# First mixer's gate projection in seven half-size products; norm weights as columns; one pair's k products placed later

## The chip, the cores and the metric

The kernel runs on one core of a Trainium2 chip. Its engines run side by side, each through its own list of instructions in order: TensorE (PE: matrix products; PEld is the load of its stationary operand), VectorE (DVE), ScalarE (ACT), GpSimd (POOL) and SyncE (SP, which here only issues transfers). They wait for one another through semaphores. The metric is the device time of one execution in microseconds, as the median of several runs.

## The reference

Two residual layers over 512 tokens of width 1024, in float32. Layer 0 mixes tokens by gated linear attention (the first mixer), layer 1 by gated DeltaNet (the second mixer). Behind each mixer stands a convolutional feed-forward network, and behind each of these four parts a layer normalisation. What matters here is the first mixer:

```python
def gla_mixer(x, w_in, w_gk2, b_gk, norm_w, w_out):
    proj = x @ w_in                       # 1024 -> 512 + 512 + 1024 + 1024 + 16
    q, k, v, gate, gk_lr = jnp.split(proj, ...)
    ...
    o = rms_norm(gla_chunked(qc, kc, vc, gc), norm_w)     # 4 heads of 256; norm_w has 256 numbers
    o = from_head_chunks(o).astype(x.dtype)
    return (o * jax.nn.silu(gate)) @ w_out
```

The second mixer ends in the same way, with 8 heads of 128 and a norm weight of 128 numbers. It also forms k k^T per head, and from that a triangular inverse in chunks.

## The kernel before, in words

**Precision.** A float32 product is made of three products in a faster format (fp32r). Each operand is split into a high part (`wh`, `xh`, `yh`: a cast on ScalarE) and a low part (`wl`, `xl`, `yl`: the difference to the cast, on VectorE), both by `split_out` (L591, recorded at L592). Then high x high, high x low and low x high go into one accumulator (`tm_terms`). A matmul of the large projections has a stationary operand of 128x128 and a moving one of 128x512.

**Weights.** A plan lists the weight pieces in the order of use. Each piece is a tile of 128x1024 (two blocks of 128 rows by 512 columns), loaded by SP's queue into one of three buffers named `raw`, and split into one of four pairs `wh`, `wl`. The look-ahead says how many pieces are split before they are used: two in most stages.

**The first mixer.** The projections come in the order q and k per head, then v, then the gates, then the output projection. For v and for the gates, `x_tm` calls `tm_half` once per half of the 1024 columns: four accumulators, one for each 128 tokens, and four pieces of weights; each piece is used in 24 matmuls (4 token blocks, 2 row blocks, 3 terms). That is 192 matmuls for the gates. When a block is complete, `gates` (L984) takes silu on ScalarE (L991) and multiplies by the norm weight on VectorE (L993), which lies repeated on all 128 partitions as `gla_nw`. `finish` (L1198), one task per half, waits for four gate tiles `sg` and two heads, multiplies each gate tile with the heads' output and its inverse norm (L1207, 128x256 at a time), and hands them to `split_y` (L976): four transposes per tile on TensorE (`yT`), and the split into `yh` and `yl`. These are the stationary operands of the output projection.

**The order.** The code is a recorder: one main thread issues the large projections, and after each group of matmuls `pump` resumes those side tasks whose time by an estimated clock has come. A task is `spawn`ed with a delay. A scheduler behind it keeps each engine's dependencies. So a changed delay or an added task moves instructions on an engine, not only in the text.

**A form that the kernel has elsewhere.** The output projections of the feed-forward networks are computed in the Strassen-Winograd manner, here called fold: the matrices are cut in two by two quarters, seven products of sums of quarters replace eight, and the names `b11`, `b21`, `t1`, `t2`, `b22`, `t3`, `t4` are the quarters or sums of the weights, `a11`, `a12`, `w1`, `v2`, `v4`, `v3`, `a22` those of the other operand.

**The second mixer's k.** The projections of the heads come by pairs; `k_done` (L1352) runs the convolution of a k head, and for each pair spawns `k_task`: the products k k^T (`pg`: four matmuls of 128x128 per head), with a delay of `CONV_DELAY` (6.0), and `FIRST_CONVS` (2.0) more for the first two pairs. From `pg`, through `am`, comes the inverse: a long chain on VectorE, then `dinvt` in DRAM, from which SP loads tiles `T` for the products `V`.

Of the kernel before, what the change touches and what calls it, by code (L numbers as in the profile page):

```python
# [15 lines left out]
P = 128  # L16
D = 1024
S = 512
# [12 lines left out]
FOLD = [(n, FOLD_NEW[n], *FOLD_ALL[n]) for n in ("b11", "b21", "t1", "t2", "b22", "t3", "t4")]  # L31
LN_EPS = 1e-5
# [3 lines left out]
GROUPS = ((0, 8), (8, 16), (16, 22))  # L36
SLOTS = 45
# [26 lines left out]
class Trunk:  # L64
# [3 lines left out]
    def __init__(self, ctx, tc):  # L68
# [15 lines left out]
        self.stage("gla", SLOTS)  # L84
# [24 lines left out]
        self.late = []  # L109
# [151 lines left out]

    @staticmethod
    def in_slots(item):
        return item[0] == "tm" and item[5]

    def issue(self, item):
# [6 lines left out]
        if item[0] == "fold":  # L273
            return self.issue_fold(*item[1:])
        raw = self.rp.tile([P, 1024], F32, name=self.uid("raw"), tag="raw")
# [8 lines left out]
        else:  # L284
            _, w, row, n, col, _ = item
            used = n * S
            nc.sync.dma_start(
# [15 lines left out]
        if self.issued == 0:  # L303
            self.pieces = [lambda cols=cols: split(cols) for cols in pieces]
        elif self.issued < 4:
            self.opening(*split(pieces[0]))
        else:
            parts = split(pieces[0])
            for ins, other in zip(parts, self.after):
                self.behind(ins, other)  # L310
# [64 lines left out]

    def prefetch(self):
# [9 lines left out]
    def load_ahead(self, until):  # L386


        self.loaded = max(self.loaded, self.issued)
        while self.loaded < min(len(self.plan), until) and self.plan[self.loaded][0] == "fold":  # L390
            _, group, _, quarter, i = self.plan[self.loaded]
            if quarter:
                self.fold_load(group, quarter, i)
            self.loaded += 1
# [249 lines left out]
    def load_x(self, x):  # L644
# [44 lines left out]
        def second():  # L689
# [5 lines left out]
            for t, row in self.late:  # L695
                nc.gpsimd.tensor_copy(t[:, :1], self.xl[:, NC - 1, S - 1:].bitcast(F32))
                nc.gpsimd.dma_start(t, row.partition_broadcast(P))

# [277 lines left out]
    def split_y(self, y, hf, sg):  # L976
        for tb in range(NTB):
# [3 lines left out]
            self.split_out(*t, ps)  # L981
            self.set(("y", tb, hf), 1.5)

    def gates(self, nw, width, sg):  # L984

        nc = self.nc
        r = S // width
        for hf in range(2):
            def done(tb, ps, hf=hf):
                t = self.slot("sg")  # L990
                nc.scalar.activation(t, ps, AF.Silu)  # L991
                t3 = t.rearrange("p (r d) -> p r d", r=r)
                nc.vector.tensor_mul(t3, t3, nw.unsqueeze(1).to_broadcast([P, r, width]))  # L993
# [6 lines left out]
    def gla_plan(self, w_in, w_out):  # L1000
# [5 lines left out]
        for base in (1024, 2048):  # L1006
            for hf in range(2):
                for cp in range(NC // 2):
                    self.plan_tm(w_in, 2 * cp * P, 2, base + hf * S)
        self.plan_out(w_out, 0, NC, TAIL)  # L1010

    def gla_consts(self, w_gk2, b_gk, norm_w):
# [16 lines left out]
        self.gla_nw = self.own([P, 256], "gla_nw")  # L1029
        self.late.append((self.gla_nw, norm_w))  # L1030
# [9 lines left out]
        self.spawn(self.columns([(b_gk.rearrange("(n p) -> n p", p=P), 4, self.b_gk)]), 12.0)  # L1040

    def gla(self, li, g, b):
# [155 lines left out]
        def finish(hf):  # L1198
            for tb in range(NTB):
# [3 lines left out]
            for tb in range(NTB):  # L1203
# [5 lines left out]
            yield 2.4  # L1209
            self.split_y(y, hf, sg)  # L1210

        for hd in range(GH):
            self.spawn(core(hd))
        for hf in range(2):
# [5 lines left out]
            self.x_tm(v_done)  # L1220
        for hf in range(2):
            self.spawn(finish(hf))
        self.gates(self.gla_nw, 256, sg)
# [26 lines left out]
    def gdn_consts(self, conv_w, a_log, dt_bias, norm_w):  # L1250
# [3 lines left out]
        self.gdn_nw = self.keep([P, P], "gdn_nw")  # L1254
        self.late.append((self.gdn_nw, norm_w))
# [15 lines left out]
    def gdn(self, li, g, b):  # L1271
# [371 lines left out]
        def finish(hf):  # L1643
# [10 lines left out]
            self.split_y(y, hf, sg)  # L1654
# [13 lines left out]
        self.gates(self.gdn_nw, P, sg)  # L1668
# [79 lines left out]
```

## Time and profile before

| | |
|---|---|
| median of 3 runs | 1238.53 us (1238.46 to 1238.58) |
| the profiled execution | 1238.69 us, span 1237.0 us |
| TensorE busy | 1225.5 us, 99% of the span, 6566 matmuls |
| VectorE, ScalarE, GpSimd busy | 912.5, 587.2, 123.7 us |
| DMA | 130.72 MB, 106 GB/s on average |
| granted TensorE clock | 0.998 |

The span is that of the recorded instructions; the execution is longer by what lies around it. In the rows of a profile, L197 is the line where a matmul is recorded and L214 that of a transpose; the operand names stand as out<-in. A row of a group gives the count, the busy time and the mean duration, then the idle time before it and what ended that. A row of the timeline begins with the start and the duration. A row of windows gives, for a stretch, the busy time of PE, PEld, DVE, ACT and POOL, then the granted clock, the share of the DMA engines and GB/s. Matmuls overlap: their duration is longer than the distance from one to the next.

### The profile page before, as it was taken

The numbers are of one execution on the slowest core, as the hardware profiler recorded it, in microseconds if no ns is written. First come the engines' busy times: TensorE is split into PE (matmuls) and PEld (weight loads), VectorE is DVE, ScalarE is ACT, GpSimd is POOL, SyncE is SP. The second block draws the span as 40 slices with busy tenths as digits, with TensorE's granted clock in tenths as the row PEclk, the third lists the DMA queues.
The fourth block names the chain that finished last, engine by engine and source line by source line (L and its number), as shares of the span: only waits on it lengthen the run. The fifth ranks groups of instructions, "written<-read, shape, count | busy, mean of one in ns | idle before, by whom it ended". The sixth has DMA issues, their size and how long they took to land.

```text
span 1237.0 us, 17216 instructions
## 1 busy us (share of the span) xinstructions
PE 1225.5 (99%) x6566; PEld 1035.1 (84%) x6566; DVE 912.5 (74%) x1546; ACT 587.2 (47%) x1067; POOL 123.7 (10%) x161
## 2 busy tenths in 40 slices
PE   9999999999999999999999999999999999999997
PEld 8888888988888888888988888988988888888886
DVE  4863556589966895667599965679589966796667
ACT  4654434644434443455676545534644434443440
POOL 4000000062000000001023030100053000000000
PEclk9999999999999999999999999999999999999999
DMA  7422225342353214333264241335342263223321
GB/s 208 111 79 68 69 86 162 111 137 68 103 170 102 68 52 119 119 99 108 69 171 120 85 134 36 91 114 154 106 152 84 60 201 97 86 85 102 106 66 68
DMA packets 169410, 130.72 MB, mean 106 GB/s; under 512 B 16232, under 2 KB 139946, under 8 KB 169328
## 3 DMA queue, kind: packets, MB, share of 16 engines
q1 hardware_dynamic: 164240, 120.47, 32.8%
q0 software_dynamic: 3888, 8.50, 2.4%
q8 instruction: 51, 0.84, 0.3%
q10 hardware_dynamic: 1200, 0.66, 0.2%
q14 instruction: 31, 0.25, 0.1%
HBM read 123.82 MB, written 5.78 MB: 105 GB/s over the span
## 4 chain that ended last, share of the span: by engine, by line
PE 97%; ACT 1%; DVE 1%; DMA 0%; issue 0%; POOL 0%; SPq 0%; DVEq 0%; ACTq 0%
PE fm L197 52%; PE tm L197 23%; PE fold L197 12%; PE o L197 2%; PE xT L214 1%; PE V L197 1%; PE pq L197 1%; PE vn L197 1%; PE yT L214 1%; DMA h<-in_x_dram 0%; PE qs L197 0%; PE s L197 0%; PE ks L197 0%; PE ds L197 0%; PE sa L197 0%; PE qT L214 0%
## 5 line engine op out<-in xcount | busy, mean ns | idle before, releaser
L197 PE MATMUL fm<-xh,wh 128*128 128x512 f32 (+2 forms) x1104 | 402.3, 367 | 0.7 <-ACT xh L592 0.7
L197 PE MATMUL fm<-xl,wh 128*128 128x512 f32 (+2 forms) x1104 | 400.0, 365 | 0.0
L197 PE MATMUL fm<-xh,wl 128*128 128x512 f32 (+1 forms) x1080 | 392.8, 366 | 0.0
L592 DVE TENSOR_TENSOR wl<-raw,wh 128x1024 fp32r<-128x1024 f32 (+1 forms) x161 | 200.8, 1249 | 171.7 <-ACT wh L592 171.6
L592 ACT CAST wh<-raw 128x1024 fp32r<-128x1024 f32 (+1 forms) x162 | 168.6, 1043 | 247.8 <-PE fm L197 141.3
L197 PEld LDWEIGHTS fm<-xh,wh 128*128 128x128 f32 (+1 forms) x1104 | 206.9, 188 | 33.9 <-ACT xh L592 0.9
L197 PEld LDWEIGHTS fm<-xl,wh 128*128 128x128 f32 (+1 forms) x1104 | 207.0, 188 | 32.8 <-DVE xl L592 0.2
L197 PEld LDWEIGHTS fm<-xh,wl 128*128 128x128 f32 x1080 | 202.7, 189 | 33.0
L863 DVE SCALAR_TENSOR_TENSOR conv<-fm,ffn_cw,conv 128x511 f32<-128x511 f32 x112 | 83.5, 745 | 8.9 <-ACT conv L861 7.4
L197 PE MATMUL fold<-wh,fh 128*128 128x512 f32 x224 | 87.6, 391 | 0.0
L197 PE MATMUL fold<-wl,fh 128*128 128x512 f32 x224 | 87.4, 390 | 0.0
L197 PE MATMUL fold<-wh,fl 128*128 128x512 f32 x224 | 87.2, 389 | 0.0
L592 ACT CAST wh<-b 128x1024 fp32r<-128x1024 f32 x48 | 49.6, 1052 | 60.6 <-PE fold L197 25.8
L197 PE MATMUL tm<-wh,xh 128*128 128x512 f32 x192 | 78.2, 408 | 0.0
L197 PE MATMUL tm<-wh,xl 128*128 128x512 f32 x192 | 75.1, 391 | 0.0
L197 PE MATMUL tm<-wl,xh 128*128 128x512 f32 x192 | 74.8, 389 | 0.0
L881 ACT ACTIVATE conv<-conv 128x512 f32<-128x512 f32 x44 | 27.8, 632 | 80.7 <-DVE conv L863 80.7
L790 POOL TENSOR_TENSOR h<-h,gb 128x512 f32<-128x512 f32 x16 | 28.2, 1783 | 334.2 <-DMA gb<-in_ln_g_dram 227.9
L592 DVE TENSOR_TENSOR wl<-b,wh 128x1024 fp32r<-128x1024 f32 x48 | 57.8, 1218 | 2.3 <-ACT wh L592 2.3
L1266 DVE SCALAR_TENSOR_TENSOR conv<-fm,gdn_cw,conv 128x511 f32<-128x511 f32 (+2 forms) x72 | 52.7, 743 | 2.0 <-ACT conv L1264 1.5
L197 PEld LDWEIGHTS fold<-wh,fh 128*128 128x128 f32 x224 | 42.0, 188 | 9.8 <-DVE h L952 1.2
L197 PEld LDWEIGHTS fold<-wl,fh 128*128 128x128 f32 x224 | 42.0, 188 | 9.4 <-DVE wl L592 0.8
(323 smaller groups left out, 1852.7 us busy)
## 6 DMA issues: line engine op xcount, KB each, us to landing
raw<-in_ffn_w_in_dram SPq DMA_DIRECT2D x88, 512.0 KB, 3.8
raw<-in_gdn_w_in_dram SPq DMA_DIRECT2D x32, 512.0 KB, 4.1
raw<-in_ffn_w_out_dram SPq DMA_DIRECT2D x28, 512.0 KB, 3.7
b<-in_ffn_w_out_dram SPq DMA_DIRECT2D x24, 512.0 KB, 4.9
raw<-in_gla_w_in_dram SPq DMA_DIRECT2D x23, 512.0 KB, 3.7
raw<-in_gla_w_out_dram SPq DMA_DIRECT2D x8, 512.0 KB, 3.6
raw<-in_gdn_w_out_dram SPq DMA_DIRECT2D x8, 512.0 KB, 3.8
h<-in_x_dram SPq DMA_DIRECT2D x8, 256.0 KB, 5.8
```

The source lines that it names most:

```text
L197: t = self.nc.tensor.matmul(out, a, b, start=start, stop=stop, skip_group_check=joined)
L214: t = self.nc.tensor.transpose(out, a, self.ident[:n, :n])
L592: return self.nc.scalar.copy(dst_h, src), self.nc.vector.tensor_sub(dst_l, src, dst_h)
L790: nc.gpsimd.tensor_mul(h[hf], h[hf], gb[hf])
L863: nc.vector.scalar_tensor_tensor(a[:, d:], ps[:, :S - d], tap(2 - d), a[:, d:], ALU.mult, ALU.add)
L881: nc.scalar.activation(a, a, AF.Gelu)
L1266: self.conv = nc.vector.scalar_tensor_tensor(a[:, d:], ps[:, :S - d], tap(3 - d), a[:, d:], ALU.mult, ALU.add)
```

## The change

**Gates of the first mixer.** `x_tm` is replaced by `gated`, the seven products on x and the gate weights: tokens in two halves of 256, rows of the weight in even and odd pairs of blocks, columns in two halves of 512. Each product has two pieces of weights, 14 in all, and each piece serves 12 matmuls (2 token blocks, 2 row blocks, 3 terms): 168 matmuls. Two pairs of accumulators (named `fold`) are used in turn, with `t2`, `t3` adding onto what `b11`, `t2` left, and `t4` onto `t3`. The tiles `gw` keep the running sums of weights; `t1`, `t2`, `t3`, `t4` are made by VectorE (L410 to L415). `x_forms` is a new side task that makes `w1`, `v2`, `v4`, `v3` out of x beside the v projection. `update` carries results from the accumulators to gate tiles, by copies on ScalarE and sums on VectorE. The look-ahead in this stage is 3.

**Norm weights.** They become columns, one number per partition, and are applied in `split_y` behind the transposes: `yh` is a multiplication on ScalarE, `yl` one operation on VectorE. For the first mixer these go by halves of 256, 16 of each; the multiplications at L993 are gone in both mixers. Two copies and two broadcasts on GpSimd go; two rows more are transposed by tiny matmuls. The two weight tiles keep their old size, so that what is allocated after them keeps its address modulo 1024 bytes.

**Finish.** One task per half and pair of token blocks, four instead of two.

**The k products.** The longer delay holds for the third pair too.

```diff
+GATED = (("b11", "a11", 0), ("b21", "a12", 1), ("t1", "w1", 1), ("t2", "v2", 0), ("b22", "v4", 1), ("t3", "v3", 0),
+         ("t4", "a22", 0))
+GLA_SLOTS = 47
...
+    def issue_gated(self, group, name, i):
+        t = group.pop((name, i))
...
+        if name in ("t1", "t2"):
+            nc.vector.tensor_add(total, total, t)
+            t = total
+        elif name == "t3":
+            nc.vector.tensor_sub(t, total, t)
+        elif name == "t4":
+            nc.vector.tensor_add(t, total, t)
...
+        self.split_out(wh, wl, t)
...
-    def split_y(self, y, hf, sg):
-        for tb in range(NTB):
+    def split_y(self, y, hf, sg, nw, blocks=range(NTB)):
+        for tb in blocks:
...
-            self.split_out(*t, ps)
+            n = nw.shape[1]
+            view = lambda a, i: a.rearrange("p (c n i) -> p n c i", n=n, i=P)[:, i]
+            for i in range(n):
+                yh, yl, src = (view(a, i) for a in (*t, ps))
+                nc.scalar.mul(yh, src, nw[:, i:i + 1])
+                nc.vector.scalar_tensor_tensor(yl, src, nw[:, i:i + 1], yh, ALU.mult, ALU.subtract)
...
+    def x_forms(self, forms):
...
+        def full(odd, tok):
+            ts = [self.slot("xq") for _ in range(2)]
+            for k, t in enumerate(ts):
+                self.behind(nc.vector.tensor_add(pair(t), *(part(x, odd, tok, k) for x in (self.xh, self.xl))),
+                            self.split[1])
+            return ts
...
+    def gated(self, sg, forms):
+        acc = [[self.psum("fold") for _ in range(2)] for _ in range(2)]
...
+        def update(name, r):
+            p, x = acc[0][r], acc[1][r]
+            if name == "b11":
+                top[r] = copied(p)
+            elif name == "b21":
+                nc.vector.tensor_add(top[r], top[r], x)
+                done(r, 1, top[r], top[r])
+            elif name == "t1":
+                high[r] = copied(x)
+            elif name == "t2":
+                right[r] = copied(p)
+            elif name == "b22":
+                nc.vector.tensor_sub(right[r], x, right[r])
+                done(r, 0, right[r], right[r])
+            elif name == "t3":
+                nc.vector.tensor_sub(high[r], high[r], p)
+                done(2 + r, 0, high[r], high[r])
+            elif name == "t4":
+                done(2 + r, 1, self.slot("sg"), p)
...
-                t3 = t.rearrange("p (r d) -> p r d", r=r)
-                nc.vector.tensor_mul(t3, t3, nw.unsqueeze(1).to_broadcast([P, r, width]))
...
-        for base in (1024, 2048):
-            for hf in range(2):
-                for cp in range(NC // 2):
-                    self.plan_tm(w_in, 2 * cp * P, 2, base + hf * S)
+        for hf in range(2):
+            for cp in range(NC // 2):
+                self.plan_tm(w_in, 2 * cp * P, 2, 1024 + hf * S)
+        self.plan_gated(w_in, 2048)
...
-        self.gla_nw = self.own([P, 256], "gla_nw")
-        self.late.append((self.gla_nw, norm_w))
+        self.gla_nw = self.own([P, 256], "gla_nw")[:, :2]
...
-                delay = CONV_DELAY + (FIRST_CONVS if hd < HEADSTART else 0.0)
+                delay = CONV_DELAY + (FIRST_CONVS if hd < HEADSTART + 2 else 0.0)
```

**What moves.** On TensorE near the end of the gates, before the change, the four transposes of the first half (`yT`) stand together between two groups of gate matmuls, at the start of the second half's second piece:

```order
L197 MATMUL tm_1426<-wl_1354,xh 128x512
L197 MATMUL tm_1426<-wh_1353,xl 128x512
L214 MATMUL yT_1465<-ident_86,sg_1393 128x128 x4
L214 MATMUL yT_1474<-ident_86,sg_1402 128x128 x4
L214 MATMUL yT_1483<-ident_86,sg_1411 128x128 x4
L214 MATMUL yT_1492<-ident_86,sg_1420 128x128 x4
L197 MATMUL tm_1423<-wh_1383,xh 128x512
L197 MATMUL tm_1423<-wl_1384,xh 128x512
```

After it, these rows stand within the second piece of t3 (its weights are `wh_1551`, `wl_1552`), and t4 (`wh_1570`) follows on the same accumulator `fold_1235` six matmuls later:

```order
L200 MATMUL fold_1235<-wh_1551,xfl_1462 128x512
L217 MATMUL yT_1625<-ident_86,sg_1540 128x128 x4
L217 MATMUL yT_1636<-ident_86,sg_1548 128x128 x2
L200 MATMUL fold_1236<-wh_1551,xfh_1461 128x512
L217 MATMUL yT_1636<-ident_86,sg_1548 128x128 x2
L200 MATMUL fold_1236<-wl_1552,xfh_1461 128x512
L200 MATMUL fold_1236<-wh_1551,xfl_1462 128x512
L200 MATMUL fold_1236<-wh_1551,xfh_1461 128x512
L200 MATMUL fold_1236<-wl_1552,xfh_1461 128x512
L200 MATMUL fold_1236<-wh_1551,xfl_1462 128x512
L200 MATMUL fold_1235<-wh_1570,xh 128x512
```

Transposes now come for two token blocks at a time, eight for each task of `finish`, and an accumulator is taken up again soon after it was completed.

On VectorE at the same place, before the change, gate tiles (`sg`) and splits of weights (`wl`) alternate in this way:

```order
L592 TENSOR_TENSOR wl_1564<-raw_1561,wh_1563 128x1024
L592 TENSOR_TENSOR wl_1610<-raw_1607,wh_1609 128x1024
L993 TENSOR_TENSOR sg_1573<-sg_1573,gla_nw_146 128x512
L1207 SCALAR_TENSOR_TENSOR sg_1573<-o_1227,gla_rr_735,sg_1573 128x256
L1207 SCALAR_TENSOR_TENSOR sg_1573<-o_1260,gla_rr_735,sg_1573 128x256
```

After it, the queue that the transposes `yT_1625` and `yT_1636` and the first matmul of t4 wait for reads as follows (`gw` and `raw` are weights being summed, L1129 and L1132 the updates from the accumulators):

```order
L644 TENSOR_TENSOR wl_1571<-raw_1532,wh_1570 128x1024
L1129 TENSOR_TENSOR sg_1540<-fold_1237,sg_1540 128x512
L1129 TENSOR_TENSOR sg_1548<-fold_1238,sg_1548 128x512
L415 TENSOR_TENSOR raw_1555<-gw_1110,raw_1555 128x1024
L1375 SCALAR_TENSOR_TENSOR sg_1540<-o_1013,gla_rr_734,sg_1540 128x256
L1375 SCALAR_TENSOR_TENSOR sg_1540<-o_1050,gla_rr_734,sg_1540 128x256
L1375 SCALAR_TENSOR_TENSOR sg_1548<-o_1013,gla_rr_734,sg_1548 128x256
L644 TENSOR_TENSOR wl_1592<-raw_1555,wh_1591 128x1024
L1375 SCALAR_TENSOR_TENSOR sg_1548<-o_1050,gla_rr_734,sg_1548 128x256
L644 TENSOR_TENSOR wl_1614<-raw_1611,wh_1613 128x1024
L1132 TENSOR_TENSOR sg_1477<-sg_1477,fold_1235 128x512
```

So updates, weight sums and weight splits now stand between the operations that make a gate tile ready for its transposes.

On TensorE in the second mixer, the products `pg` of the third pair stood behind the first six matmuls of the next projection:

```order
L197 MATMUL fm_5305<-xl,wh_5203 128x512
L197 MATMUL fm_5305<-xh,wl_5204 128x512
L197 MATMUL pg_5312<-conv_5195 128x128 x4
L197 MATMUL pg_5321<-conv_5232 128x128 x4
L197 MATMUL fm_5305<-xh,wh_5203 128x512
```

Now they stand behind twelve:

```order
L200 MATMUL fm_5399<-xl,wh_5297 128x512
L200 MATMUL fm_5399<-xh,wl_5298 128x512
L200 MATMUL pg_5412<-conv_5289 128x128 x4
L200 MATMUL pg_5421<-conv_5326 128x128 x4
L200 MATMUL fm_5399<-xh,wh_5297 128x512
```

They moved back by six matmuls; the other pairs kept their places.

More of the change, by code (lines that the diff above doesn't have):

```diff
@@ new lines, in split, with both @@
+        def split(name, ts):
+            forms[name] = []
+            for t in ts:
+                h, l = self.slot("xfh", F32R), self.slot("xfl", F32R)
+                self.split_out(h, l, t)
+                forms[name].append((h, l))
+            self.set(("form", name), 2.0)
+        def both(a, b, op, out):
+            for x, y, o in zip(a, b, out):
+                nc.vector.tensor_tensor(o, x, y, op)
+        a = full(0, 256)
+        yield 2.0
+        b = full(1, 256)
+        yield 2.0
```

146 lines of the change are left out of this document (120 added, 26 removed).

## The prediction

> **What bounds the kernel now.** I read the head of the page first, then the chain of waits, then the stretch of the first mixer's gates (about 122 to 176 us) by windows and by groups. The page:
>
> ```profile
> span 1237.0 us, 17216 instructions
> PE 1225.5 (99%) x6566; PEld 1035.1 (84%) x6566; DVE 912.5 (74%) x1546; ACT 587.2 (47%) x1067; POOL 123.7 (10%) x161
> PE 97%; ACT 1%; DVE 1%; DMA 0%; issue 0%; POOL 0%; SPq 0%; DVEq 0%; ACTq 0%
> ```
>
> TensorE is busy for 99% of the span and is 97% of the chain that ended last. So a matmul less is worth its full spacing, and anything else counts only where it makes TensorE wait. The spacing is read from start to start, in the timeline of the gates and in one of the second mixer (7 and 15 matmuls from the first row of each pair to the second):
>
> ```profile
> 160.25 0.40 PE L197 MATMUL tm<-wl,xh 128*128 128x512 f32 x1
> ...
> 161.84 0.39 PE L197 MATMUL tm<-wh,xl 128*128 128x512 f32 x1
> ...
> 717.77 0.39 PE L197 MATMUL fm<-xh,wl 128*128 128x512 f32 x1
> ...
> 721.17 0.39 PE L197 MATMUL fm<-xh,wl 128*128 128x512 f32 x1
> ```
>
> 1.59/7 = 0.227 us and 3.40/15 = 0.2267 us. The duration of 0.39 us overlaps the next one and must not be used as a price.
>
> What else is there in the gate stage, by windows (PE, PEld, DVE, ACT, POOL, each busy us with its count):
>
> ```profile
> 90.00:122.00 32.00, 32.00 (x144) 26.85 (x143) 12.30 (x43) 12.75 (x29) 0.00 (x0) 1.00 0.22 66
> 122.00:136.00 14.00, 14.00 (x66) 11.98 (x65) 6.92 (x21) 7.06 (x19) 0.00 (x0) 1.00 0.14 39
> 136.00:150.00 14.00, 14.00 (x63) 11.58 (x62) 4.55 (x16) 5.64 (x10) 0.00 (x0) 1.00 0.24 75
> 150.00:164.00 14.00, 14.00 (x72) 11.82 (x71) 10.42 (x18) 5.48 (x9) 0.00 (x0) 1.00 0.32 114
> 164.00:176.00 12.00, 12.00 (x55) 9.94 (x54) 5.64 (x9) 4.04 (x6) 0.00 (x0) 1.00 0.26 87
> ```
>
> TensorE has no gap. Over 122 to 176, VectorE is busy for 27.5 of 54 us and ScalarE for 22.2. In the 32 us ahead of it VectorE leaves 19.7 us free.
>
> **The matmuls.** The gate projection goes from 8 weight pieces of 24 matmuls (192) to 14 pieces of 12 (168): 24 x 0.2267 = 5.44 us less. Two tiny transposes for the norm weights' columns are new; the nearest row is
>
> ```profile
> L214 PE MATMUL cols<-ident,rows 4*128 4x4 f32 x1 | 0.2, 222 | 0.0
> ```
>
> so they cost between 0 (overlapped) and 0.44 us; I take +0.2, since they overlap at least partly, as all matmuls here do.
>
> Of this price the Trainium skill ("TensorE: Matmul & The Clock Gate", section "Back-to-back issue gap") says something else: about 131 ns for N=512 in a sustained stream, and N/2.4 + 2.5 = 215.8 ns for an isolated one. By the first figure the 24 matmuls would be an estimated 3.1 us and the change would fall to about 1237.0, within the noise; by the second 5.2 us. The trace disagrees with the 131 ns, at 226.7 ns over 15 matmuls in a row, so that case gets no chance.
>
> **VectorE's new work.** Prices, from the groups of the stretch 88 to 184 and one timeline row for back-to-back spacing:
>
> ```profile
> L592 DVE TENSOR_TENSOR wl<-raw,wh 128x1024 fp32r<-128x1024 f32 x13 | 15.9, 1224 | 30.0 <-ACT wh L592 30.0
> L592 ACT CAST wh<-raw 128x1024 fp32r<-128x1024 f32 x13 | 13.7, 1051 | 31.2 <-PE tm L197 31.2
> L1207 DVE SCALAR_TENSOR_TENSOR sg<-o,gla_rr,sg 128x256 f32<-128x256 f32 x16 | 6.9, 480 | 0.1
> L993 DVE TENSOR_TENSOR sg<-sg,gla_nw 128x512 f32<-128x512 f32 x8 | 5.4, 685 | 0.7 <-ACT sg L991 0.7
> L592 ACT CAST yh<-yT 128x512 fp32r<-128x512 f32 x8 | 4.1, 599 | 4.3 <-PE yT L214 4.3
> ...
> 159.99 2.48 DVE L592 TENSOR_TENSOR yl<-yT,yh 128x512 fp32r<-128x512 f32 x4
> ```
>
> Four of 128x512 take 2.48 us, 0.62 each, some 0.06 under their duration; so I count 1.16 for 128x1024, 0.62 for 128x512 and 0.42 for 128x256. Added: 6 splits of weights 7.0, 8 sums and differences of weights 9.3, 24 operations on forms of x 14.9, 6 updates of gate tiles 3.7, and the products' low parts as 16 halves instead of 8 wholes, 1.8. Removed: 8 multiplications by the norm weight, 5.0. Together +31.7 us on VectorE. By its order some 16 of the form operations and 2 sums (12.2 us) stand ahead of the first gate product, where 19.7 us are free: those cost nothing. The other 19.5 us raise the gate stage from 27.5 to 47.0 us of VectorE, in 54 - 5.4 = 48.6 us of TensorE. That is the point of this change: an engine that had half its time free now has 3% free, and what it delivers late TensorE waits for.
>
> There are three places. Before product t1, a bank must have been read by VectorE (update b21), and before t4 another (update t3); at the transposes yT, TensorE waits for gate tiles that are queued on VectorE behind splits of weights, all in order. The tightest part is the end. From t3's first matmul to the fourth block of the output projection TensorE has 66 matmuls of 128x512, 66 x 0.2267 = 15.0 us, and 24 transposes. Their price is in the timeline, 16 in 159.24 - 157.57 = 1.67 us, so 2.5 us for 24:
>
> ```profile
> 157.57 1.91 PE L214 MATMUL yT<-ident,sg 128*128 128x128 f32 x16
> ...
> 159.24 0.48 PE L197 MATMUL tm<-wh,xh 128*128 128x512 f32 x1
> ```
>
> In all 17.5 us. VectorE has 32 operations there: 8 splits and 2 sums of 128x1024 (11.6), 4 updates (2.5), 18 halves (7.6), 21.7 us. It is short by 4.2 us, less what it has done ahead. With three weights split ahead (the lookahead of the stage) that is 3.5 us, with one 1.2 us: it waits for 0.7 to 3.0 us. The lower bound is 0, because the fold stage of the first channel mixer shows a full VectorE under a full TensorE:
>
> ```profile
> 331.00:342.00 11.00, 11.00 (x49) 8.80 (x48) 11.00 (x14) 5.51 (x6) 0.00 (x0) 1.00 0.75 236
> ```
>
> That stage also alternates sums, splits and products, but has no gate tile that must come back to TensorE within 4 us; so it is the nearer row for the banks and not for yT. I take the middle, +1.5, and keep 0 and 3.0.
>
> ScalarE gets 6 casts of 1.05, 8 casts and 6 copies of 0.6, and products by the norm weight in halves (about 1 us): 22.2 + 15.7 = 38 of 48.6 us. It is no bound. GpSimd loses two small copies and two broadcasts that nothing on the chain waits for: 0. In the second mixer 8 multiplications leave VectorE beside the gates; TensorE does not wait there: 0. That tiles keep their sizes, so that operands stay at equal addresses modulo 1024, I cost at 0: the spacing above is the same in two stages whose operands lie differently.
>
> **The weight loads.** The gates take 14 loads of 512 KB instead of 8, all on SP's queue, and the loads of the output projection stand behind them. Landing times by group:
>
> ```profile
> raw<-in_gla_w_in_dram SPq DMA_DIRECT2D x23, 512.0 KB, 3.7
> b<-in_ffn_w_out_dram SPq DMA_DIRECT2D x24, 512.0 KB, 4.9
> ...
> gb<-in_ln_g_dram SPq DMA_DIRECT2D x4, 256.0 KB, 6.4
> T<-dinvt SPq DMA_DIRECT2D x12, 32.0 KB, 2.5
> ```
>
> A buffer is held for the landing, a sum 1.2, a cast 1.05 and a split 1.2: 3.7 + 3.4 = 7.1 us, with three buffers 2.4 us per weight. TensorE uses a weight up in 12 x 0.2267 = 2.72 us. So they are hidden, by 0.3 us per weight: cost 0. With the 4.9 us of the denser loads it would be 2.8 us, 0.05 to 0.1 us late each, about +1 in all.
>
> Against the change speaks the Trainium skill ("DMA: Bandwidth & Descriptors", section "Issuing engines are not separate DMA queues"): transfers from all queues run on the same 16 engines and interleave. The trace agrees, as far as 4.9 against 3.7 us for the same size shows it. By that rule with the dense figure, the estimate would be 1 us more than mine.
>
> **The third pair's k products.** TensorE stands still for them once in the second mixer:
>
> ```profile
> 629.20 1.16 PE L197 MATMUL pg<-conv 128*128 128x128 f32 x8 [1.03 <-ACT conv L1268]
> ```
>
> They move six matmuls, 1.36 us, later, which covers the 1.03 us. But VectorE is full afterwards, and what it prepares is the inverse that V needs:
>
> ```profile
> 650.00:662.00 12.00, 12.00 (x59) 10.01 (x58) 12.00 (x52) 11.29 (x23) 7.85 (x15) 1.00 0.21 38
> ...
> 700.00:714.00 14.00, 14.00 (x74) 11.90 (x73) 13.59 (x33) 6.79 (x24) 2.96 (x6) 1.00 0.24 76
> ...
> 712.41 0.74 DVE L1266 SCALAR_TENSOR_TENSOR conv<-fm,gdn_cw,conv 128x509 f32<-128x509 f32 x1
> ...
> 719.44 0.92 SPq L1443 DMA_DIRECT2D T<-dinvt x2
> ...
> 721.49 1.36 PE L197 MATMUL V<-T,am 32*32 32x32 f32 x32
> ```
>
> The second of these loads of T is issued at about 719.9 and lands 2.5 us later, at 722, while V is under way: there is no slack. A TensorE that is 1.0 us earlier at V waits 1.0 us more. In VectorE's order one convolution (0.74 us) also comes to stand ahead in that chain. The ends are -1.0 (kept) and +0.7; by the full windows I take -0.1.
>
> **Sum.** -5.44 + 0.2 + 1.5 - 0.1 = -3.84 us. The profiled execution took 1238.69 us (span 1237.0 and 1.7 around it), which gives 1234.85; the median of the runs, 1238.53, is 0.16 lower, so 1234.7. The low end is -5.44 - 1.0 = -6.4, 1232.1; the high end -5.44 + 0.44 + 3.0 + 0.7 = -1.3, 1237.2, and 1238.2 with late loads.
>
> **Rivals.**
> A, everything is hidden: lookahead keeps VectorE ahead, as in the fold stage. Then only -5.44 + 0.2 and perhaps part of the 1.03 us: 1232.1 to 1233.4. Against it speak the 3% that VectorE has left.
> B, VectorE is the bound of the gates: it enters t3 with one weight or none ahead and TensorE waits 3 us there, and another 0.5 to 1 at t1's bank. 1236.1 to 1238.2, no change that could be told (0.2% is 2.5 us, about what a measurement here can tell from none).
> C, slower: the loads set the pace. The buffer cycle must then cost more than the 5.44 us saved and 2.5 beyond it, 8 us over 12 loads that turn around, 0.67 each: 3.39 us per weight, 10.2 us per buffer, so a landing of 6.8 us, just above the 6.4 us row. The time is then 1241 or more. The share of DMA engines in these windows (0.14 to 0.32) speaks against it.
> D, the k products change more than their 1.03 us, the chain to V being later by a convolution: +0.7 instead of -0.1, 1235.5. That lies within the likeliest case.
>
> **Chances.** The likeliest (with D), 1233.4 to 1236.05: 0.58. A 0.16, B 0.15, C 0.11. Faster by over 0.2% is below 1236.05: 0.58 + 0.16 = 0.74; within it 0.15; slower 0.11. The range 1232.3 to 1237.4 leaves out C, some third of B (0.05) and a sliver of A: 0.17.
>
> **What would show it.** After: 168 matmuls for the gates at 0.227 us; VectorE above 90% from the first product to the output projection; idle time on TensorE's yT and on the first matmul of t1 or t4, released by VectorE, 1 to 2 us together; loads of the gates landing in under 4.5 us; no idle time at pg and about 1 us at V, released by the loads of T. Wrong would be: gaps of over 3 us in the gate stage, a wait of the cast for a load, or a V more than 1 us later than pg's gain explains.

## The result and the profile after

| | before | after |
|---|---|---|
| median, 14 runs each | 1238.81 us (1238.35 to 1240.38) | 1236.41 us (1235.76 to 1237.7) |
| ratio, 95% interval | | 0.9981 (0.9973 to 0.9988) |
| profiled execution, span | 1238.69, 1237.0 us | 1236.11, 1234.4 us |

The changed kernel is 0.19% faster. The interval excludes 1, but the gain is just under the 0.2% that the prediction took as the least that can be told, and it is 2.4 us where 3.8 were forecast. From the page of the changed kernel, its head and its chain:

```profile
span 1234.4 us, 17236 instructions
PE 1220.7 (99%) x6544; PEld 1029.6 (83%) x6544; DVE 936.1 (76%) x1584; ACT 602.8 (49%) x1095; POOL 123.8 (10%) x159
PE 88%; DVE 7%; ACT 1%; DMA 1%; issue 1%; POOL 0%; SPq 0%; DVEq 0%; ACTq 0%
```

TensorE is 4.8 us less busy, but the span is only 2.6 us shorter. The chain that ended last has 7% of VectorE in it, where it had 1%.

The same instruction in both traces shows where the gain went. The first is the first large matmul of the kernel, the second the first one of the feed-forward network behind the first mixer, the third the start of V in the second mixer. From before:

```profile
7.98 0.73 PE L197 MATMUL fm<-xh,wh 128*128 128x256 f32 x4
...
222.78 0.28 PE L197 MATMUL fm<-xh,wh 128*128 128x256 f32 x1
```

and from after:

```profile
7.75 0.74 PE L200 MATMUL fm<-xh,wh 128*128 128x256 f32 x4
...
218.53 0.28 PE L200 MATMUL fm<-xh,wh 128*128 128x256 f32 x1
```

At the end of the first mixer the changed kernel is 4.25 us ahead, of which 0.23 were there at the first matmul. V starts at 718.60 instead of 721.49 us (the prediction has the row of before): 2.89 us ahead. At the last matmul it is 2.67 us. So the gates gave 4.0 us, and on the way to the last matmul 1.6 us of it were given back, all but 0.2 of that by V.

The 4.0 us can be split further. The gates begin with these rows, before and after:

```profile
121.64 0.39 PE L197 MATMUL tm<-wh,xh 128*128 128x512 f32 x1
```

```profile
121.76 0.39 PE L200 MATMUL fold<-wh,xh 128*128 128x512 f32 x1
```

From there to the feed-forward network it is 101.14 us before and 96.77 after, 4.37 less. So of the 5.44 us of 24 matmuls, 1.07 are lost from the first gate product on, and 0.35 more ahead of the gates.

In the gates, by windows:

```profile
122.00:136.00 14.00, 14.00 (x65) 12.02 (x64) 10.44 (x21) 9.93 (x23) 0.00 (x0) 1.00 0.25 77
136.00:150.00 14.00, 14.00 (x66) 11.11 (x65) 13.52 (x38) 11.09 (x20) 0.00 (x0) 1.00 0.19 43
150.00:164.00 14.00, 14.00 (x66) 11.43 (x64) 13.48 (x19) 9.22 (x15) 0.00 (x0) 1.00 0.58 183
164.00:172.00 8.00, 7.87 (x39) 6.27 (x39) 7.90 (x14) 5.63 (x11) 0.00 (x0) 1.00 0.59 197
```

VectorE is busy for 45.3 of 50 us (91%), and from 136 us on for 34.9 of 36 (97%). TensorE has hardly a gap. What it waits for from 122 to 172 us, by the list of waits (total, times, longest; PEld is the load of the stationary operand):

```profile
PEld yT L217 <- DVE sg L1375: 0.6, 2, 0.3
PEld fold L200 <- DVE sg L1132: 0.6, 1, 0.6
PEld fold L200 <- DVE wl L644: 0.2, 1, 0.2
PEld fold L200 <- DVE sg L1122: 0.2, 1, 0.2
```

These are the places that the prediction named: yT behind the gate tiles, t4's accumulator (L1132), t1's (L1122). In the timeline, counted as what the distance from start to start exceeds the usual one, 0.45 us stand at yT, 0.41 at t4's accumulator and 0.14 at t1's. The second mixer, in TensorE's timeline and the first row of VectorE's:

```profile
624.33 1.95 PE L200 MATMUL pg<-conv 128*128 128x128 f32 x16
...
654.70 0.66 PE L217 MATMUL vT<-ident,conv 128*128 128x128 f32 x4 [0.33 <-ACT conv L1440]
...
661.01 0.50 PE L200 MATMUL fm<-xh,wl 128*128 128x512 f32 x1 [1.08 <-DVE wl L644]
...
718.60 0.69 PE L200 MATMUL V<-T,am 32*32 32x32 f32 x16 [0.67 <-DMA T<-dinvt]
719.53 0.69 PE L200 MATMUL V<-T,am 32*32 32x32 f32 x16 [0.25 <-DMA T<-dinvt]
```

```profile
630.42 0.17 DVE L1552 TENSOR_SCALAR gd_bp<-gd_ssq 128x4 f32<-128x4 f32 x1 [1.63 <-ACT dg L1548]
```

The wait of 1.03 us at pg is gone; all 16 records run in one piece (the program's float32 products pg, four per head, stand as two records each). Four new waits stand behind it, 2.3 us together. And VectorE stands for 1.63 us at gd_bp, the small operation that follows pg, where it stood 0.27 us before:

```profile
633.22 0.17 DVE L1380 TENSOR_SCALAR gd_bp<-gd_ssq 128x4 f32<-128x4 f32 x1 [0.27 <-ACT dg L1376]
```

### The profile page after: what moved, and what is told of

The parts are those of the page before. It is cut to its first block, busy times and chain, and to the rows that moved or that the text cites. A ratio compares the mean times of both kernels' runs of the same rounds, so it can differ in the third digit from the quotient of the medians.

```text
span 1234.4 us, 17236 instructions
## 1 busy us (share of the span) xinstructions
PE 1220.7 (99%) x6544; PEld 1029.6 (83%) x6544; DVE 936.1 (76%) x1584; ACT 602.8 (49%) x1095; POOL 123.8 (10%) x159
## 4 chain that ended last, share of the span: by engine, by line
PE 88%; DVE 7%; ACT 1%; DMA 1%; issue 1%; POOL 0%; SPq 0%; DVEq 0%; ACTq 0%
PE fm L200 46%; PE tm L200 20%; PE fold L200 15%; DVE conv L1438 2%; PE o L200 2%; PE xT L217 1%; DVE wl L644 1%; DVE tt L1598 1%; DVE am L1557 1%; DVE tmp L1596 1%; PE vn L200 1%; PE V L200 1%; PE yT L217 1%; ACT dg L1548 0%; DVE dt L1501 0%
## 5 line engine op out<-in xcount | busy, mean ns | idle before, releaser
L1438 DVE SCALAR_TENSOR_TENSOR conv<-fm,gdn_cw,conv 128x509 f32<-128x509 f32 (+2 forms) x72 | 52.7, 743 | 2.3 <-ACT conv L1436 1.9
L200 PE MATMUL tm<-wh,xh 128*128 128x512 f32 x128 | 52.6, 411 | 0.0
L200 PE MATMUL tm<-wh,xl 128*128 128x512 f32 x128 | 50.1, 391 | 0.0
L200 PE MATMUL tm<-wl,xh 128*128 128x512 f32 x128 | 49.9, 390 | 0.0
```

What stands on the lines that cost most here:

```text
L200: t = self.nc.tensor.matmul(out, a, b, start=start, stop=stop, skip_group_check=joined)
L1438: self.conv = nc.vector.scalar_tensor_tensor(a[:, d:], ps[:, :S - d], tap(3 - d), a[:, d:], ALU.mult, ALU.add)
```

## The experiments

In each group of runs the kernel before was run on the same chip, and the ratio is to it. Where ratios are close, the traces decide.

### The delay taken back, and the delay alone

```diff
-                delay = CONV_DELAY + (FIRST_CONVS if hd < HEADSTART + 2 else 0.0)
+                delay = CONV_DELAY + (FIRST_CONVS if hd < HEADSTART else 0.0)
```

on the changed kernel:

> The changed kernel with the third pair's k products back at their old delay. Theory (the delay costs more than it saves: it makes the first of the two products pg 1.36 us later for VectorE, which is full from 650 us on, and TensorE pays at a weight split, at vT and at V): the waits at the weight split near 661 us (1.24 us) and at V (1.0 us) are gone, the wait of 1.0 us at pg is back, and the median falls from 1236.4 to about 1234.9 (1234.6 to 1235.4). Rival (the waits come from another part of the change, or from the gates being earlier): they stay, the wait at pg comes on top, and the median is 1236.4 to 1237.5. The prediction on record would have it at 1236.5, 0.1 above.

and the reverse edit on the kernel before:

> The kernel before with the longer delay of the third pair's k products alone. Theory (the delay costs): 1.2 to 1.6 us slower than before, 1240.0 to 1240.4, with new waits at a weight split near 665 us and at V. The prediction on record: 0.1 us faster, between -1.0 and +0.7. Rival (the waits come from the other parts): no change or up to 1 us faster, the pg wait being gone.

The theory held in both. Without the delay: 1235.01 us (1234.4 to 1235.58), ratio 0.9960 (0.9948 to 0.9973); the median is 1.4 us under that of the changed kernel, by the ratios it is 2.6, and between the two traces 1.0 us. With the delay alone: 1241.41 us, ratio 1.0016 (1.0008 to 1.0025), slower by 2.0 us, and by 2.4 in the trace, which is more than the 1.2 to 1.6 expected. Without it, TensorE's timeline reads

```profile
623.21 1.05 PE L200 MATMUL pg<-conv 128*128 128x128 f32 x8
625.29 1.16 PE L200 MATMUL pg<-conv 128*128 128x128 f32 x8 [1.03 <-ACT conv L1440]
...
717.64 1.30 PE L200 MATMUL V<-T,am 32*32 32x32 f32 x32
```

with pg's old wait, and V in one piece without a wait on its row. With the delay alone, the kernel before gets the wait at the split:

```profile
665.28 0.50 PE L197 MATMUL fm<-xh,wl 128*128 128x512 f32 x1 [1.10 <-DVE wl L592]
```

So the delay costs, in both kernels, and the rest of the change does not cause these waits. The kernel without the delay has the lowest ratio of this study. It is faster than the kernel before; its interval (to 0.9973) ends where that of the changed kernel begins.

### Which part of the delay

```diff
-                self.spawn(k_task(hd), delay)
+                self.spawn(k_task(hd), delay + (2.5 if hd == HEADSTART + 1 else 0.0))
```

with the first product back at its place; the second alone stands six matmuls later.

> The changed kernel in which, of the third pair's two k products, only the second stands six matmuls later; the first is back at its old place. Ratios to before so far: changed 0.9981, without the delay 0.9960. Theory (what costs is that the first product is late for ScalarE and VectorE; the second has to wait for its convolution in any case, and its move only fills that wait): the 1.0 us wait at pg goes, no wait at the weight split near 661 us and none over 0.5 us at V, ratio 0.9950 to 0.9954 (1.0 us less than without the delay, 0.2 given back for one more switch of TensorE). Rival (the chain to V needs the second product too, or VectorE's order is at fault): ratio 0.9960 or more, with a wait of 1 us at V in place of that at pg.

1235.47 us, ratio 0.9974 (0.9965 to 0.9983); in the trace its end is 0.05 us from that of the kernel without the delay. The gain at pg was there, 1.46 us by then, and was lost again, the largest part at one place:

```profile
696.82 0.66 PE L217 MATMUL qT<-ident,conv 128*128 128x128 f32 x4 [1.22 <-ACT conv L1440]
```

So the expectation was wrong: moving the second product does not only fill a wait. By the ratio its rival is nearer, but the new wait stands at qT and not at V. VectorE stood 1.33 us at the second product's gd_bp. The next theory was that this standing is the loss, and that VectorE could do other work in the meantime. Two kernels put gd_bp behind the last k head's convolution in VectorE's list (in the first for both products, both late; in the second for the second product, the only late one):

```diff
+            if hd == 7:
+                self.last_k = self.conv
+                self.set(("kc", 7), 0.0)
...
+            if hd in (4, 5):
+                yield from self.until(("kc", 7))
-            nc.vector.tensor_scalar_add(bp[:, hd, :], ssq[:, 1, hd, :], RMS_EPS)
+            eps = nc.vector.tensor_scalar_add(bp[:, hd, :], ssq[:, 1, hd, :], RMS_EPS)
+            if hd in (4, 5):
+                self.behind(eps, self.last_k)
```

> The changed kernel, both k products of the third pair late as in it, but the small VectorE operations that wait for them (gd_bp) are placed behind the last k head's convolution in VectorE's list. Theory (the loss is VectorE standing 1.6 us at gd_bp, ahead of a stretch where it is full; what stands behind it in order is late from there on): VectorE does the convolution and a weight split in that time, the waits of TensorE near 661 us and at V shrink by about 1.6 us together, the one at pg stays gone, and the ratio to before is 0.9950 to 0.9960, against 0.9981 for the changed kernel. Rival (what costs is the lateness of the chain from the products to the inverse itself, whatever VectorE does meanwhile): the waits move to V, ratio 0.9975 to 0.9985.

> The kernel in which only the second k product of the third pair is late, and its gd_bp alone stands behind the last k head's convolution. Theory as before: VectorE's wait of 1.3 us there goes, with it TensorE's wait of 1.2 us at the transposes qT; ratio 0.9950 to 0.9957, 1 us better than without the delay (0.9960) and than with the second product late but gd_bp in front (0.9974, profiled 1235.2 us). Rival: VectorE's total work from 640 to 715 us sets V, so the gain at pg is lost at V: as without the delay, 0.9960 to 0.9970.

> The changed kernel once more, beside the two kernels with gd_bp moved and the same runs of before, so that they are compared on one chip: 0.9975 to 0.9988, with waits at the weight split near 661 us and at V.

The first: 1241.15 us, ratio 1.0018 (1.001 to 1.0027). The second: 1236.79, 0.9978 (0.9969 to 0.9987). The changed kernel beside them: 1236.39, 0.9980 (0.9971 to 0.9989). The theory fell: the first of the two is 4.8 us slower than the changed kernel, the second no faster than it. In the first VectorE does not stand at gd_bp any more, but longer at the convolution:

```profile
632.48 1.53 DVE L1438 SCALAR_TENSOR_TENSOR conv<-fm,gdn_cw,conv 128x511 f32<-128x511 f32 x2 [3.37 <-ACT conv L1436]
```

It waits there for ScalarE's part of the convolution (L1436), and in ScalarE's list that part stands behind the eight operations on the diagonal `dg` of the late products, with no idle time between them (the first and the last of the eight, then L1436):

```profile
629.42 0.32 ACT L1551 ACTIVATE dg<-dg 128x128 f32<-128x128 f32 x1
...
631.48 0.30 ACT L1551 ACTIVATE dg<-dg 128x128 f32<-128x128 f32 x1
...
631.77 0.67 ACT L1436 ACTIVATE conv<-fm,gdn_cw 128x512 f32<-128x512 f32 x1
```

The cast `wh`, which VectorE's next weight split needs, stands behind that (632.35). In the changed kernel, too, L1436 follows the eight directly, at 631.46 us. So moving gd_bp alone gave VectorE nothing to do in the meantime; a kernel in which ScalarE's list is changed as well was not tried. What remains is read from one window, 626 to 634 us, in the changed kernel, without the delay, and with gd_bp moved (one row from each):

```profile
626.00:634.00 8.00, 8.00 (x38) 6.66 (x37) 5.68 (x18) 5.02 (x21) 1.27 (x2) 1.00 0.67 174
```

```profile
626.00:634.00 8.00, 8.00 (x39) 6.68 (x38) 6.86 (x19) 5.45 (x21) 1.26 (x2) 1.00 0.73 197
```

```profile
626.00:634.00 8.00, 8.00 (x40) 6.70 (x39) 4.52 (x11) 5.32 (x21) 1.26 (x2) 1.00 0.77 208
```

VectorE is idle there for 2.3, 1.1 and 3.5 us; behind it, it is nearly full up to V (in the changed kernel busy for 68.9 of 70 us from 644 to 714). Beside it, what TensorE waits behind this window up to V, by the lists of waits:

| kernel | VectorE idle, 626 to 634 | TensorE waits, 632 to 725 | where |
|---|---|---|---|
| without the delay | 1.1 us | none on the list | |
| second product late | 1.6 us | 1.7 us | vT, qT |
| the same, its gd_bp moved | 2.1 us | 1.6 us | vT, V |
| changed kernel | 2.3 us | 2.3 us | vT, split, V |
| both gd_bp moved | 3.5 us | 5.7 us | vT, split, V |

More idle time ahead of the full stretch goes with more waits behind it, except that the second and third rows differ by 0.1 us the other way; where the waits fall differs. That fits a VectorE whose work up to V is fixed. In the last row the chain to V is late by itself as well (gd_bp is part of it), and an estimated 3.4 of its 4.8 us come from a halved clock behind V (6.8 us of it, of which more at the end); so it does not separate the two. That the k products' lateness is what costs is shown by the runs with and without the delay; that it works through VectorE's idle time is an agreement over five kernels, not more.

### The gates: VectorE's load

```diff
         if name in ("t1", "t2"):
-            nc.vector.tensor_add(total, total, t)
-            t = total
+            group["sum", i] = t
-        elif name == "t3":
-            nc.vector.tensor_sub(t, total, t)
         elif name == "t4":
-            nc.vector.tensor_add(t, total, t)
```

> The changed kernel without the eight sums and differences of gate weights: each of the 14 pieces is split as loaded, so that four of the seven products use other weights than they should and the gates come out differently; all loads, splits and matmuls stay. It takes 9.3 us of VectorE out of the gates. Theory (TensorE's waits in the gates come from VectorE being 97% busy): the waits at the splits, at yT and at t4's accumulator, 0.6 to 0.9 us of spacing beyond what a switch costs, go: ratio 0.9973 to 0.9977 against 0.9981. Rival (these gaps are the price of switching between products and transposes, and of accumulators read in turn): unchanged, 0.9980 to 0.9983.

1237.14 us (1236.37 to 1239.11), ratio 0.9990 (0.9981 to 0.9999), which is no faster. But the trace tells the gates apart from a thing that happened at V, of which more below. The first matmul behind the first mixer:

```profile
218.15 0.28 PE L200 MATMUL fm<-xh,wh 128*128 128x256 f32 x1
```

From the same start (7.97 us) the changed kernel, in its second profile, is there at 218.77: 0.6 us are saved. Of the waits above, those at yT, at t4's accumulator and at the split are gone; the one at t1's accumulator has grown from 0.2 to 0.5 us by the list. So in the gates the theory holds, at the lower end of its size (0.6 to 0.9), while by the ratio alone it would have failed.

```diff
-        self.look = 3
+        self.look = 2
```

> The changed kernel with a look-ahead of 2 weight pieces in the gates instead of 3. Theory (VectorE's lead of up to three split pieces is what covers its shortfall of 4.2 us near the end of the gates): the lead is 1.2 us shorter and TensorE waits 0.5 to 1.2 us more, ratio 0.9985 to 0.9991. Rival (gate tiles are served sooner if fewer splits stand ahead of them in VectorE's queue): 0 to 0.7 us faster, 0.9975 to 0.9981.

1236.7 us, ratio 0.9985 (0.9977 to 0.9994). In the trace the same matmul starts at 218.73 us: no difference in the gates. That says nothing of the lead, because the edit is not the one that was meant: this `look = 3` (L1003) belongs to the output projections of the feed-forward networks, and the one in `gated` (L1137) was left as it was. In the two traces the instructions of VectorE and ScalarE up to the end of the first mixer are the same ones in the same order. So whether three pieces in hand cover anything in the gates was not tested. For the stage that was changed, no difference can be told: the intervals of 0.9985 and 0.9981 overlap.

```diff
-            nc.vector.tensor_add(total, total, t)
+            nc.gpsimd.tensor_add(total, total, t)
```

and likewise for the other sums:

> The changed kernel with the eight sums and differences of gate weights on GpSimd instead of VectorE. Theory (VectorE, 13.5 of 14 us busy from 136 to 164, is what TensorE waits for in the gates): VectorE loses 8 x 1.16 = 9.3 us there, the waits of TensorE at yT, at a weight split and at t4's accumulator (about 0.9 us together) go, and the median falls by 0.5 to 1.0, to 1235.4 to 1235.9. Rival (the sums become late): at 1.87 us for 128x512 on GpSimd a sum takes about 3.7 us, 2.5 longer than on VectorE; the pieces of t1 to t4 then come too late for a look-ahead of 3 x 2.72 us, and the median is above 1237.

1247.18 us, ratio 1.0056 (1.0042 to 1.0069): 10.5 us later at the end of the trace, nearly all of it in the gates. The rival held. A sum takes 2.4 to 3.2 us on GpSimd, and a split on VectorE that begins while one runs becomes longer:

```profile
158.03 3.22 POOL L413 TENSOR_TENSOR raw<-gw,raw 128x1024 f32<-128x1024 f32 x1 [12.31 <-DMA raw<-in_gla_w_in_dram]
```

```profile
159.31 3.03 DVE L644 TENSOR_TENSOR wl<-raw,wh 128x1024 fp32r<-128x1024 f32 x1 [0.33 <-ACT wh L644]
```

against 1.22 us for a split in the changed kernel. The sum ends at 161.25 us, the split 1.09 us behind it. The other split that begins during a sum (at 167.01 us, 2.65 long) also ends 1.09 us behind that sum, and the splits that begin before one take 1.22 to 1.23 us. The Trainium skill ("SBUF — State Buffer", section "SBUF: two separate sides") says that GpSimd and a VectorE instruction with two inputs in SBUF share a pair of ports, which the one that starts first holds until it ends. The trace agrees with it: a split has two inputs, and here it ends as if it had begun when the sum was over. The waits then cost twice, because the clock fell:

```profile
143.57 0.50 PE L200 MATMUL fold<-wl,xfh 128*128 128x512 f32 x1 [1.90 <-DVE wl L644]
146.39 0.79 PE L200 MATMUL fold<-wh,xfh 128*128 128x512 f32 x1 [2.32 <-DVE sg L1122]
146.98 0.63 PE L200 MATMUL fold<-wl,xfh 128*128 128x512 f32 x1
147.41 0.63 PE L200 MATMUL fold<-wh,xfl 128*128 128x512 f32 x1
147.84 0.63 PE L200 MATMUL fold<-wh,xfh 128*128 128x512 f32 x1
```

The spacing is 0.43 us instead of 0.227 from there to about 152 us.

### Columns alone, and other addresses

The kernel before with the new `split_y`, the columns and without the multiplications at L993; its other lines are as they were:

```diff
-            self.split_out(*t, ps)
+            for i in range(n):
+                yh, yl, src = (view(a, i) for a in (*t, ps))
+                nc.scalar.mul(yh, src, nw[:, i:i + 1])
+                nc.vector.scalar_tensor_tensor(yl, src, nw[:, i:i + 1], yh, ALU.mult, ALU.subtract)
...
-                nc.vector.tensor_mul(t3, t3, nw.unsqueeze(1).to_broadcast([P, r, width]))
```

> The kernel before with the norm weights as columns alone (scalar multiplications in place of casts behind the transposes, no multiplications of gate tiles, two small transposes more), without the seven products and without the delay. Prediction on record: 0 to +0.44 us for the transposes, 0 for the rest, so ratio 0.9998 to 1.0004. Rival (the halves of 256 make yh and yl late for the output projection, or GpSimd's copies and broadcasts had cost something at the start): more than 1 us either way.

1239.28 us, ratio 1.0004 (0.9995 to 1.0013); at the last matmul of the trace it is 0.40 us behind, 0.2 of it by the end of the first mixer. Its first large matmul came 0.13 us earlier than in the kernel before, so counted from there it is 0.53 us, a little over the upper bound. This part gains nothing, as forecast; that the loss is that of the two transposes was not shown.

```diff
-        self.gla_nw = self.own([P, 256], "gla_nw")[:, :2]
+        self.gla_nw = self.own([P, 2], "gla_nw")
...
-        self.gdn_nw = self.keep([P, P], "gdn_nw")[:, :1]
+        self.gdn_nw = self.keep([P, 1], "gdn_nw")
```

> The changed kernel with the two norm weight tiles at their own small size (2 and 1 columns), so that all tiles allocated after them lie at other addresses: the operands of about 1460 matmuls are no longer equal modulo 256 bytes. Theory on record (addresses cost nothing): spacing 0.227 us everywhere and 1236.4 within 0.5. Rival (the operands' addresses modulo 1024 matter): a longer spacing in the matmuls whose moving and stationary operands differ by 480, 992, 448 or 224 bytes, and a median above 1238; 10 ns more for each of 1460 would be 15 us.

1243.27 us (1241.29 to 1245.05), ratio 1.0027 (1.0018 to 1.0036), against 0.9981: 5.7 us slower by the ratios, with the same instructions. The trace is 5.4 us longer, spread over many stages. One of them here, and the same one in the changed kernel:

```profile
446.05 0.40 PE L200 MATMUL fold<-wh,fl 128*128 128x512 f32 x1
...
449.55 0.40 PE L200 MATMUL fold<-wh,fl 128*128 128x512 f32 x1
```

```profile
442.82 0.39 PE L200 MATMUL fold<-wh,fl 128*128 128x512 f32 x1
...
446.22 0.39 PE L200 MATMUL fold<-wh,fl 128*128 128x512 f32 x1
```

15 matmuls take 3.50 instead of 3.40 us: 233.3 ns each, not 226.7. The traces hold no addresses; they are those that the built program gives its tiles. Sorted by them modulo 256 over the whole trace, the spacing is 227 ns at the median where moving and stationary operand agree (both at 128, 160 or 192) and 232 or 233 ns where they differ (128 and 160, 128 and 192; 953 matmuls): an estimate of 953 x 6 ns = 5.7 us. In the changed kernel all 128x512 products of fp32r agree. The rival was right, at half the size that it named, and for some 950 matmuls instead of 1460.

## Why the prediction was right, and where it was not

The median lies inside the range, and the forecast had the direction right. But it lies above the likeliest case (1233.4 to 1236.05) and in the band of rival B (1236.1 to 1238.2), whose mechanism, 3 us of waits at t3, did not come. "Faster by over 0.2%" had a chance of 0.74; it was 0.19%. What moved the result there is the last term of the sum, which went beyond its upper bound. That the total stayed inside the range is luck in so far as the waits in the gates stayed far under theirs.

- **The bound and the spacing: right.** In the changed kernel's gates, too, the spacing is 0.227 us, and 24 matmuls less gave the largest term, -5.44 us. The 131 ns that the Trainium skill gives for N=512 ("TensorE: Matmul & The Clock Gate", section "Back-to-back issue gap") were not seen.
- **VectorE's load: right.** 19.5 us more were forecast for the gates, to 97% of them. It is 45.3 instead of 27.5 us, some 18 more, to 91%; 97% holds from 136 us on. The price list held (sums 1.22, updates 0.68, halves 0.48 us as durations).
- **The waits in the gates, +1.5: right in place, a little high.** 1.07 us are lost there, and 1.0 of it stands in the timeline at the three places that the prediction named. The kernel without sums shows that the waits at yT and at t4's accumulator come from VectorE's load: with 9.3 us less of it they go, and 0.6 us are saved. The working by three weights in hand was not tested.
- **The loads: right.** The loads of this matrix still land in 3.7 us at the median (27 on the page), and the longest wait for one in the gates is 0.2 us, on VectorE. Rival C did not come.
- **Columns, GpSimd, second mixer's multiplications: about right**, +0.4 to +0.5 in the kernel with columns alone, where +0.2 was taken and 0.44 was the bound. Some 0.3 of it is the loss ahead of the gates.
- **Equal addresses, cost 0: the forecast held, its reason did not.** The kept tile sizes do keep the spacing. But "the spacing above is the same in two stages whose operands lie differently" proved nothing about other differences: in both stages the operands agreed modulo 256, and where they do not, a matmul takes 6 ns more.
- **The k products, -0.1: the step that failed.** The term was to lie between -1.0 and +0.7, on the ground that a TensorE which is earlier at V waits there. Taken back, it made the kernel 1.0 us (traces) to 2.6 us (ratios) faster; added alone, 2.0 us slower. The prediction's own sign of being wrong showed as well: with the 4.25 us of the gates and the 1.03 of pg, V would start 5.28 us earlier, and it starts 2.89 earlier, 2.4 us later than that explains. The prediction asked what TensorE would find at V, and not what VectorE would miss: it followed the moved product on the engine that issues it, but not what waits for it, the diagonal on ScalarE and gd_bp on VectorE, directly ahead of a stretch in which VectorE was shown full. Its own row of 12.00 of 12 us for VectorE was a reason to look there.

From the end of the first mixer to the last matmul the two traces lose 1.6 us (4.25 to 2.67). The kernel without the delay loses 0.4 us there too (4.06 ahead, then 3.62), so some 1.1 to 1.2 us are the delay's, in a profile without a halved clock ahead of the last few microseconds. With +1.1 for that term, +0.5 for the columns and +1.1 for the gates the sum is -5.44 + 0.5 + 1.1 + 1.1 = -2.7 us, where the traces have 2.67 and the medians 2.4.

## What to carry to other kernels

When an instruction is moved later, follow its result to the next engine and look whether that one is full behind the place. Here 1.0 us of waiting was removed, VectorE stood 1.2 us more ahead of its full stretch, and 2.3 us of new waits came on TensorE up to some 90 us later. Fewer matmuls at the price of vector work paid here, with VectorE at 91 to 97%: 24 matmuls less gave three quarters of their worth. Compare kernels of equal layout: two tiles of another size moved 950 matmuls by 6 ns each. And look in the trace whether an edit has moved anything where it was meant to.

## What the runs showed of the hardware that was not expected

**Addresses of the operands.** Above: 227 ns where both operands of a 128x512 fp32r matmul agree modulo 256 bytes, 232 to 233 ns where they differ by 32 or 64. Differences of 256, 512 and 768 cost nothing (227 ns at the median for each in the changed kernel). Why is open.

**The granted clock falls behind short waits.** The changed kernel was profiled twice. In the second profile its waits at V were nearly the same, but the clock was halved behind them (windows around V, first the first profile, then the second):

```profile
719.00:725.00 6.00, 5.75 (x110) 4.36 (x109) 4.04 (x7) 2.31 (x5) 6.00 (x12) 1.00 0.43 72
```

```profile
719.00:725.00 6.00, 5.78 (x44) 4.47 (x44) 3.90 (x5) 1.88 (x4) 6.00 (x13) 0.72 0.47 75
```

```profile
719.01 0.69 PE L200 MATMUL V<-T,am 32*32 32x32 f32 x16 [0.66 <-DMA T<-dinvt]
719.91 0.69 PE L200 MATMUL V<-T,am 32*32 32x32 f32 x16 [0.21 <-DMA T<-dinvt]
...
721.34 0.63 PE L200 MATMUL fm<-xh,wl 128*128 128x512 f32 x1
721.77 0.63 PE L200 MATMUL fm<-xh,wh 128*128 128x512 f32 x1
722.20 0.63 PE L200 MATMUL fm<-xl,wh 128*128 128x512 f32 x1
```

Some eight matmuls at 0.427 instead of 0.227 us, 3.4 us in all, cost an estimated 1.7 us; that execution took 1238.06 us, the other 1236.11. The kernel without sums, the one with gd_bp of the second product moved and the one with both moved have the same behind V (seven, six and some twelve matmuls). By the traces' record of the clock it is halved for 3.41 us in three of these four profiles and for 6.83 in the last. Five other profiles with waits at V do not have it, and the four without such waits (before, without the delay, second product late, columns alone) do not have it either. The Trainium skill ("TensorE: Matmul & The Clock Gate", section "Part 1: The HAM clock gate") gives a free-running window of about 3.4 us in which activity is judged. The length of the slow stretch agrees, and so does that the same waits lead to it in one execution and not in another. Its table names an idle window of that length as the condition of the slow clock; here waits of 0.66 and 0.21 us around 32 tiny matmuls stood ahead of it, with no idle time as long as that. So a wait there can cost more than its length. Of 25 timed executions of the changed kernel seven are above 1237.0 us. In the later group the three of them have a granted clock of 0.997 and the other eight 0.998 or 0.999, which fits a slow stretch; in the first group the four have 0.998 or 0.999 like the rest, so there it is not the reason, and what is stays open.
